# Two blocks of weights side by side: a decoder trunk whose half tiles change from 1024 rows of one block to 512 rows of two

## The chip, the cores and the metric

The kernel runs on one core of one Trainium2 chip. The metric is the device time of one execution in microseconds (us), the median of several runs. Matrix products run on TensorE, which reads weights and features from SBUF (the on-chip memory of 128 partitions) and adds into PSUM; VectorE and ScalarE do the elementwise work; SyncE (SP) issues the DMA transfers that bring the weights from HBM.

## What is computed

Two layers of a decoder trunk over 256 positions of width 2048, batch 1, in float32. Every product `a @ w` below is one of the matrix products that the change touches, save the small ones per pair of heads.

```
for l in range(DEPTH):                      # DEPTH = 2
    u = rms_norm(x, g_mix[l])
    cq_raw, ckv_raw, xb, yb, gate_a, gate_r = split_columns(u @ w_in[l])
    attn = mla_branch(cq_raw, ckv_raw, ...) # 16 heads, in 8 groups of two
    rec = rglru_branch(xb, yb, ...)         # conv, gates, a scan over positions, gelu
    merged = sigmoid(gate_a) * attn + sigmoid(gate_r) * rec
    x = x + merged @ w_out[l]
    hdn = square(relu(rms_norm(x, g_mlp[l]) @ w_up[l]))      # 8192 wide
    x = x + hdn @ w_down[l]
    x = x + sigmoid(rms_norm(x, g_ple[l]) @ w_ple_gate[l]) * (p[l] @ w_ple_proj[l])
return rms_norm(x, g_final)
```

## The kernel before

Features lie on the partitions and the 256 positions along the free axis. A feature tile is 128 features; the stream of 2048 is 16 such tiles (k = 0 to 15). Each activation is held twice, as a rounded part and the rest, side by side for each k in the buffers bufA and bufB; which buffer holds what alternates by stage. A weight is split in the same way, and three matmuls stand for one product of 128 x 128 weights with 256 positions: rounded x rounded, rounded x rest, rest x rounded (`mm3`, L221 to L223).

The weights come as one stream of 1,004 half tiles of 128 x 1024 (512 KB each), in the order in which they are used. A half tile of the large products holds 8 of the 16 k of one block of 128 output features. `load` (L102) issues one DMA for each on SP's queue into one of six raw buffers; `load_to` runs eight half tiles ahead of use, as far as buffers are free. `split_half` (L116) lets ScalarE round it (hi, L122) and VectorE take the rest (lo, L126), two half tiles ahead of use.

`mm_pair` computes two blocks into one PSUM bank of 512 columns, 256 for each. It takes four half tiles, `mm_half` 24 matmuls for each: first both halves of block 0, then both of block 1. For the first pair of most stages (`crossed`) the order is k 0 to 7 for block 0, the same for block 1, then k 8 to 15 for each, as the last features of the stage before come late. The last pair of a stage that must finish block by block goes through `mm_apart`, and single half tiles (the per-head projections, the embedding projection) are used as they are.

A small planner sets the order of everything else while the program is built: `later` enters a job (steps on VectorE, ScalarE, GpSimd with an estimated cost), `work` emits those that fit ahead of an estimated TensorE time, `need` forces a job when a matmul wants its result. Hooks between the half tiles of a pair place the norm's row sums (`root`, plain float32 matmuls into ms, L502), the broadcast of the norm's factor (`spread`, a plain float32 matmul into rb, L551) and the attention of the group before.

Stages per layer: c and kr (compressed queries and keys), 8 groups of xb, yb, gr, k, v, q, qr, lru, ga with the attention steps s, pt, o; then out (the output projection, whose input is merged by L1015 to L1024), four times up and down (the MLP), pp and pg (the embedding gate). In the profile's lines the tile written by a matmul has these names.

Of the kernel before, what the change touches and what calls it, by code (L numbers as in the profile page):

```python
# [18 lines left out]
P = 128  # L19
S = 256  # L20
D = 2048
KT = D // P
DEPTH = 2
HEADS = 16
GROUPS = HEADS // 2
D_FF = 8192
CHUNKS = D_FF // D
# [49 lines left out]
def trunk_kernel(ctx: ExitStack, tc: tile.TileContext, xT, pT, pos, par, gfin, invf, wu, out):  # L77
# [21 lines left out]
    nxt = {"dma": 0, "half": 0, "used": 0}  # L99
    LA, PD = 2, 8  # L100

    def load(h):  # L102
        t = wraw.tile([P, 1024], F32, tag="raw", name=f"raw{h}")
        nc.sync.dma_start(out=t, in_=wu[h])
        raws[h] = t

    def load_to(h):
# [75 lines left out]
    def need(key):  # L183

        if key not in done:
            next(j for j in jobs if key in j.keys).force()
        E["P"] = max(E["P"], done[key] + LATENCY)
# [31 lines left out]
    def mm3(o, wh, wl, ah, al, start, stop, shared=False):  # L219

        T.matmul(o, lhsT=wh, rhs=ah, start=start, stop=False, skip_group_check=shared)  # L221
        T.matmul(o, lhsT=wh, rhs=al, start=False, stop=False, skip_group_check=shared)  # L222
        T.matmul(o, lhsT=wl, rhs=ah, start=False, stop=stop, skip_group_check=shared)  # L223
        E["P"] += 0.328

    def mm_half(o, act, s, first=True, shared=False):


        hi, lo = half()
        for kk in range(8):  # L230
            k = 8 * s + kk
            need((act[1], k))
            c = slice(kk * P, (kk + 1) * P)
            mm3(o, hi[:, c], lo[:, c], act[0][:, k, 0, :], act[0][:, k, 1, :], first and k == 0, k == 15, shared)

    readers = {}

# [14 lines left out]
        for i in range(2):  # L252
            mm_half(ps[:, 0:S], act, i)

    def mm_pair(name, key, act, hooks=(), crossed=False):


        ps = mm_bank(name, key)
        for i in range(4):
            t, s = (i % 2, i // 2) if crossed else (i // 2, i % 2)  # L260
            mm_half(ps[:, t * S:(t + 1) * S], act, s, t == 0, True)
            if i < len(hooks) and hooks[i] is not None:
                hooks[i]()
        return ps
# [367 lines left out]
    def mixer(l, u, mg, norm):  # L632
        nl = Norm(f"c{l}", 512, 2, norm)
        raw, cn = {}, {}

        def dest(i, pr):
            raw[i, pr] = att.tile([P, 512], F32, tag="qk"[i] + "hl"[pr], name=f"raw{i}{pr}_{l}")
            return raw[i, pr]


        hooks = {1: (norm.root, None, None, norm.spread)} if l else {2: (None, norm.root), 3: (norm.spread,)}
        for n in range(4):
            i, pr = divmod(n, 2)
            key = ("c", i, pr, l)
            ps = mm_pair(f"c{i}{pr}_{l}", key, u, hooks.get(n, ()), n == 0)
            later(key, ("A", 0.6, lambda i=i, pr=pr, ps=ps: A.activation(dest(i, pr), ps, AF.Copy)), rank=-1)
            if l == n == 0:
                rope_tables()
                lru_constants()
            nl.squares((nl.name, "sq", n), lambda i=i, pr=pr: raw[i, pr], i, deps=(key,), last=pr == 1)  # L650


        kr = {}
        ps_k = mm_bank(f"kr_{l}", ("kr", l))
        mm_tile(ps_k, u)

        def evac_kr():
            kr["y"] = att.tile([P, S], F32, tag="oT", name=f"ykr_{l}")
            V.tensor_tensor(out=kr["y"], in0=ps_k[:, 0:S], in1=norm.R, op=ALU.mult)

        later(("kr", l), ("V", 0.38, evac_kr), deps=norm.factor(), rank=0)

        def normed():
            def steps(i, pr):
                d = {}

                def scale():
                    if i not in cn:
                        cn[i] = tuple(att.tile([P, 4, S], F32R, name=f"c{i}{w}_{l}", tag=f"c{i}{w}") for w in ("hi", "lo"))
                    d["v"] = raw[i, pr]  # L670
                    for t in range(2):
                        V.scalar_tensor_tensor(
                            out=d["v"][:, t * S:(t + 1) * S], in0=d["v"][:, t * S:(t + 1) * S],
                            scalar=param(l, ("g_q", "g_kv")[i], 2 * pr + t), in1=nl.R[:, i * S:(i + 1) * S],
                            op0=ALU.mult, op1=ALU.mult,
                        )

                def high():
                    A.activation(pair_of(cn[i][0], pr), d["v"], AF.Copy)

                def low():
                    V.tensor_tensor(out=pair_of(cn[i][1], pr), in0=d["v"], in1=f(pair_of(cn[i][0], pr)), op=ALU.subtract)

                return ("V", 0.8, scale), ("A", 0.52, high), ("V", 0.6, low)

            for i in (1, 0):
                for pr in range(2):
                    later(("cn", l, i, pr), *steps(i, pr), deps=nl.factor(), rank=0)

        def rot_kr():  # L690
            def sw():
                if "sw" not in kr:
                    kr["sw"] = t256(f"sw_k{l}")
                return kr["sw"]

            def split(d):
                return split_steps(d, f"krk{l}", lambda: d["t"], "kr", S)

            kr["rot"] = rotated(("rot", f"k{l}"), f"k{l}", lambda: kr["y"], lambda: kr["y"], sw, ("rope", ("kr", l)), split)

        def spread():
            nl.spread()
            normed()

        first = (nl.root, None, None, spread)
        for g in range(GROUPS):
            first = group(l, g, u, mg, norm, cn, kr, first, rot_kr if g == 0 else None)
# [334 lines left out]
    def residual(name, act, after):  # L1042

        def add(ps, xs):
            V.tensor_tensor(out=xs, in0=ps, in1=xs, op=ALU.add)

        for pr in range(8):
            if pr < 7:
                keys = (f"{name}_{pr}",)
                ps = mm_pair(f"{name}_{pr}", keys[0], act, (), pr == 0)  # L1050
                later(keys[0], ("V", 0.65, lambda ps=ps, pr=pr: add(ps, pair_of(x, pr))), rank=-1)
            else:
                keys = tuple((f"{name}_{pr}", t) for t in range(2))
                for t, ps in mm_apart(f"{name}_{pr}", keys, act):
                    later(keys[t], ("V", 0.38, lambda ps=ps, t=t: add(ps, x[:, 14 + t, :])), rank=-1)
            if after is not None:
                after(pr, keys)

    def mlp(l, a, hid, norm, after):
        for c in range(CHUNKS):  # L1060
            h_ = (hid, f"hid{l}_{c}")
            for pr in range(8):
                nm = f"{l}_{c}_{pr}"
                if c == CHUNKS - 1 and pr in (1, 5):
                    (ple_fetch, ple_rows)[pr // 5](l)
                ps_u = mm_pair(f"up{nm}", ("up", nm), a, BOUNDARY.get(8 * c + pr, lambda n: ())(norm), pr == 0)

                def steps(ps, pr, nm):
                    h, lo = parts(hid, pr)
# [30 lines left out]
    def ple(l, a, norm, after, hooks, by_tile=None):  # L1100
        need(("pe", l))
        ph, pl = (pe_in[w].rearrange("p (a s) -> p a s", s=S) for w in "hl")
        for pr in range(8):
# [42 lines left out]
                    after(pr, keys)  # L1146
            else:
                hook = BOUNDARY[pr](norm) if pr < 2 else hooks(pr)
                ps = mm_pair(f"pg{nm}", ("pg1", nm), a, hook, pr == 0)
                scale, tanh, mul, add = steps(ps, pps[pr % 2], pair_of(x, pr), lambda nm=nm: t512(f"pgt{nm}"))  # L1150
                later(("pg1", nm), ("V", 0.65, scale), deps=norm.factor(), rank=0)
                later(("pg", nm), ("A", 0.52, tanh), ("V", 0.6, mul), ("V", 0.6, add), deps=(("pg1", nm),))
# [227 lines left out]
```

## Time and profile before

| | us |
|---|---|
| median of 3 runs | 2925.97 (2925.73 to 2928.0) |
| profiled execution | 2925.61 |
| its span, first to last instruction | 2923.8 |
| TensorE busy (share of the span) | 2898.5 (99%) |
| VectorE busy | 1860.8 (64%) |
| ScalarE busy | 1536.2 (53%) |
| DMA, mean over the span | 183 GB/s |

The profile is one execution. Its busy times count an engine as busy from the start of an instruction to its modelled end, so for pipelined matmuls the distance between two starts says more than the duration of one. A stretch of the span is given by its start and end in us from the first instruction.

### The profile page before, as it was taken

To read this page: it belongs to the slowest core of one execution; us is meant where nothing else is said; L and a number is where in the kernel's file an instruction comes from. 1 tells how busy PE (TensorE), PEld (TensorE's weight loads), DVE (VectorE), ACT (ScalarE), POOL (GpSimd) and SP (SyncE) were. 2 spreads that over 40 slices of the span, in tenths; PEclk is the share of its full clock that TensorE was granted. 3 is DMA by queue.
4 is the path that set the end of the run, shared out by engine and by line. 5 is a ranking of instruction groups with operands and counts; after the bars stand their busy time and mean duration, and the time that the engine had idled before them with its cause. 6 is when DMAs were issued, how large, how long until landed. Compare 5 with 4: busy or idle time off the path is not lost. (4 is left out here: it accounts for less than half of the span.)

```text
span 2923.8 us, 58376 instructions
## 1 busy us (share of the span) xinstructions
PE 2898.5 (99%) x24800; PEld 2893.3 (99%) x24800; DVE 1860.8 (64%) x2420; ACT 1536.2 (53%) x2050; POOL 8.9 (0%) x17
## 2 busy tenths in 40 slices
PE   8999999999999999999999999999999999999998
PEld 8999999999999999999999999999999999999998
DVE  7877777765455554556758777777654555555565
ACT  5666666644344443444546666665443444434445
POOL 0000000000000000000000000000000000000000
PEclk9999999999999999999999999999999999999999
DMA  6555555555555555555555555555555555555553
GB/s 236 172 179 175 170 177 177 177 195 185 185 187 187 188 187 187 189 186 186 194 182 172 173 174 175 179 180 176 193 187 185 186 187 187 188 188 190 186 183 130
DMA packets 146998, 535.23 MB, mean 183 GB/s; under 512 B 16560, under 2 KB 16816, under 8 KB 146736
## 3 DMA queue, kind: packets, MB, share of 16 engines
q1 hardware_dynamic: 146736, 531.50, 55.2%
q8 instruction: 194, 3.18, 0.4%
q14 instruction: 68, 0.56, 0.0%
HBM read 529.33 MB, written 2.10 MB: 182 GB/s over the span
## 5 line engine op out<-in xcount | busy, mean ns | idle before, releaser
L122 ACT ACTIVATE hi<-raw 128x1024 fp32r<-128x1024 f32 x1004 | 1065.3, 1061 | 1358.5 <-PE down L222 412.0
L126 DVE TENSOR_TENSOR lo<-raw,hi 128x1024 fp32r<-128x1024 f32 x1004 | 1229.2, 1224 | 863.7 <-ACT hi L122 862.2
L221 PE MATMUL down<-bufB,hi 128*128 128x256 f32 x1024 | 287.7, 281 | 0.0
L222 PE MATMUL down<-bufB,hi 128*128 128x256 f32 x1024 | 287.7, 281 | 0.0
L223 PE MATMUL down<-bufB,lo 128*128 128x256 f32 x1024 | 287.7, 281 | 0.0
L221 PE MATMUL down<-bufA,hi 128*128 128x256 f32 x1024 | 287.7, 281 | 0.0
L222 PE MATMUL down<-bufA,hi 128*128 128x256 f32 x1024 | 287.7, 281 | 0.0
L223 PE MATMUL down<-bufA,lo 128*128 128x256 f32 x1024 | 287.7, 281 | 0.0
L221 PE MATMUL up<-bufA,hi 128*128 128x256 f32 x1024 | 287.7, 281 | 0.0
L221 PE MATMUL up<-bufB,hi 128*128 128x256 f32 x1024 | 287.7, 281 | 0.0
L223 PE MATMUL up<-bufA,lo 128*128 128x256 f32 x1024 | 287.5, 281 | 0.0
L223 PE MATMUL up<-bufB,lo 128*128 128x256 f32 x1024 | 287.5, 281 | 0.0
L222 PE MATMUL up<-bufA,hi 128*128 128x256 f32 x1024 | 287.5, 281 | 0.0
L222 PE MATMUL up<-bufB,hi 128*128 128x256 f32 x1024 | 287.5, 281 | 0.0
L222 PEld LDWEIGHTS down<-bufB,hi 128*128 128x128 f32 x1024 | 196.6, 192 | 0.0
L222 PEld LDWEIGHTS down<-bufA,hi 128*128 128x128 f32 x1024 | 196.6, 192 | 0.0
L222 PEld LDWEIGHTS up<-bufB,hi 128*128 128x128 f32 x1024 | 196.4, 192 | 0.0
L222 PEld LDWEIGHTS up<-bufA,hi 128*128 128x128 f32 x1024 | 196.4, 192 | 0.0
L221 PEld LDWEIGHTS up<-bufA,hi 128*128 128x128 f32 x1024 | 192.2, 188 | 0.0
L221 PEld LDWEIGHTS up<-bufB,hi 128*128 128x128 f32 x1024 | 192.2, 188 | 0.0
L223 PEld LDWEIGHTS up<-bufA,lo 128*128 128x128 f32 x1024 | 192.2, 188 | 0.0
L221 PEld LDWEIGHTS down<-bufB,hi 128*128 128x128 f32 x1024 | 192.2, 188 | 0.0
(551 smaller groups left out, 7839.1 us busy)
## 6 DMA issues: line engine op xcount, KB each, us to landing
raw<-wu SPq DMA_DIRECT2D x1004, 512.0 KB, 3.4
y<-rows SPq DMA_DIRECT2D x4, 512.0 KB, 4.0
x<-xT SPq DMA_DIRECT2D x3, 512.0 KB, 8.3
x<-xT SPq DMA_DIRECT2D x2, 256.0 KB, 4.9
praw<-pT SPq DMA_DIRECT2D x2, 256.0 KB, 4.7
parT<-par SPq DMA_DIRECT2D x1, 184.0 KB, 2.4
rope_w<-pos SPq DMA_DIRECT2D x1, 128.0 KB, 3.6
gf<-gfin SPq DMA_DIRECT2D x1, 8.0 KB, 8.3
```

Source lines behind the costliest of these rows:

```text
L122: A.activation(hi, src, AF.Copy)
L126: V.tensor_tensor(out=lo, in0=src, in1=f(hi), op=ALU.subtract)
L221: T.matmul(o, lhsT=wh, rhs=ah, start=start, stop=False, skip_group_check=shared)
L222: T.matmul(o, lhsT=wh, rhs=al, start=False, stop=False, skip_group_check=shared)
L223: T.matmul(o, lhsT=wl, rhs=ah, start=False, stop=stop, skip_group_check=shared)
```

## The change

A half tile of a pair now holds four k of both blocks: 512 columns of the one, 512 of the other. The array in HBM stays as it is; `plan` says for each half tile which pieces of which stored half tile it takes, and `load` issues one DMA per piece: one for the half tiles that stay as they were (`alone`), two of 256 KB for those of a pair. `mm_both` takes the place of `mm_half` in pairs: for each k, three matmuls for block 0 into columns 0 to 255, then three for block 1 into columns 256 to 511, on the same features. Every pair runs k from 0 to 15 in this order, so `crossed` goes. Only the first matmul of the bank carries the start flag, as before.

```diff
+    plan = []
+
+    def alone(n):
+        for _ in range(n):
+            plan.append(((len(plan), 0, 1024, 0),))
+
+    def pairs(n, crossed=False):
+        for _ in range(n):
+            b = len(plan)
+            for i in range(4):
+                plan.append(tuple(
+                    (b + (2 * (i // 2) + t if crossed else 2 * t + i // 2), 512 * (i % 2), 512, 512 * t) for t in range(2)
+                ))
+            crossed = False
+
+    for _ in range(DEPTH):
+        pairs(4, True)
+        alone(2)
+        for g in range(GROUPS):
+            pairs(3 if g == 0 else 2)
+            alone(4)
+            pairs(1 if g in (0, GROUPS - 1) else 2)
+            if g == GROUPS - 1:
+                alone(4)
+        pairs(7, True)
+        alone(4)
+        for _ in range(CHUNKS):
+            pairs(8, True)
+            pairs(7, True)
+            alone(4)
+        for i in range(4):
+            alone(1)
+            pairs(2 if i < 3 else 1, i == 0)
+        alone(4)
+
     def load(h):
         t = wraw.tile([P, 1024], F32, tag="raw", name=f"raw{h}")
-        nc.sync.dma_start(out=t, in_=wu[h])
+        for src, c, n, at in plan[h]:
+            nc.sync.dma_start(out=t[:, at:at + n], in_=wu[src, :, c:c + n])
         raws[h] = t
...
+    def mm_both(ps, act, i):
+
+        hi, lo = half()
+        for kk in range(4):
+            k = 4 * i + kk
+            need((act[1], k))
+            ah, al = (act[0][:, k, w, :] for w in range(2))
+            for t in range(2):
+                c = slice((4 * t + kk) * P, (4 * t + kk + 1) * P)
+
+                mm3(ps[:, t * S:(t + 1) * S], hi[:, c], lo[:, c], ah, al, k == t == 0, k == 15, True)
...
-    def mm_pair(name, key, act, hooks=(), crossed=False):
+    def mm_pair(name, key, act, hooks=()):
...
         for i in range(4):
-            t, s = (i % 2, i // 2) if crossed else (i // 2, i % 2)
-            mm_half(ps[:, t * S:(t + 1) * S], act, s, t == 0, True)
+            mm_both(ps, act, i)
             if i < len(hooks) and hooks[i] is not None:
                 hooks[i]()
```

## Rows read from the trace of the kernel before

**Rows 1.** The page's first part: busy us, share of the span, instructions.
```profile
PE 2898.5 (99%) x24800; PEld 2893.3 (99%) x24800; DVE 1860.8 (64%) x2420; ACT 1536.2 (53%) x2050; POOL 8.9 (0%) x17
```

**Rows 2.** Waits of TensorE: line, waited for, us in total, times, longest.
```profile
PE c L221 <- ACT hi L122: 8.5, 1, 8.5
...
PE out L222 <- DVE bufA L1024: 0.5, 1, 0.5
```

**Rows 3.** Table by stage: stretch, length, busy us and instructions per engine, PEclk, DMA share, GB/s.
```profile
0.00:540.00 540.00, 529.17 (x4525) 527.01 (x4526) 420.51 (x711) 354.26 (x550) 2.89 (x10) 1.00 0.55 183
540.00:650.00 110.00, 109.56 (x963) 109.36 (x962) 72.66 (x90) 55.89 (x72) 0.70 (x1) 1.00 0.57 187
650.00:1360.00 710.00, 710.00 (x6031) 709.95 (x6030) 381.11 (x372) 309.91 (x339) 0.00 (x0) 1.00 0.58 187
1360.00:1482.00 122.00, 122.00 (x1071) 121.89 (x1070) 83.58 (x106) 64.55 (x84) 1.40 (x2) 1.00 0.59 191
1482.00:1990.00 508.00, 506.08 (x4345) 504.27 (x4345) 384.79 (x605) 328.78 (x510) 1.86 (x1) 1.00 0.53 175
1990.00:2100.00 110.00, 109.47 (x964) 109.27 (x963) 72.12 (x89) 54.63 (x70) 0.70 (x1) 1.00 0.58 192
2100.00:2808.00 708.00, 708.00 (x6013) 707.95 (x6012) 380.16 (x371) 309.36 (x338) 0.00 (x0) 1.00 0.57 187
2808.00:2924.00 116.00, 104.21 (x904) 103.60 (x902) 65.91 (x79) 58.84 (x92) 1.39 (x2) 0.97 0.44 150
```

**Rows 4.** The same table for 80 us within layer 0's output projection.
```profile
560.00:640.00 80.00, 80.00 (x708) 80.00 (x707) 51.84 (x62) 42.29 (x54) 0.00 (x0) 1.00 0.59 193
```

**Rows 5.** Timeline of TensorE around the broadcast in layer 1's MLP: start us, duration us.
```profile
2102.38 0.28 PE L223 MATMUL up<-bufB,lo 128*128 128x256 f32 x1
...
2102.72 0.28 PE L223 MATMUL up<-bufB,lo 128*128 128x256 f32 x1
2102.84 0.59 PE L551 MATMUL rb_mlp<-dg_mlp,ones 128*128 128x256 f32 x2
...
2103.62 0.28 PE L221 MATMUL up<-bufB,hi 128*128 128x256 f32 x1
...
2103.97 0.28 PE L221 MATMUL up<-bufB,hi 128*128 128x256 f32 x1
```

**Rows 6.** Timeline of TensorE where the projection waits, layer 0 and layer 1.
```profile
555.55 0.28 PE L221 MATMUL out<-bufB,hi 128*128 128x256 f32 x1
556.27 0.39 PE L222 MATMUL out<-bufB,hi 128*128 128x256 f32 x1 [0.44 <-DVE bufB L1024]
...
2002.95 0.28 PE L221 MATMUL out<-bufA,hi 128*128 128x256 f32 x1
2003.76 0.39 PE L222 MATMUL out<-bufA,hi 128*128 128x256 f32 x1 [0.53 <-DVE bufA L1024]
```

**Rows 7.** Timeline of VectorE: the last step of the merged features 14 and 15.
```profile
555.80 0.75 DVE L1024 SCALAR_TENSOR_TENSOR bufB<-ga,bufB 128x256 fp32r<-128x256 f32 x2
```

**Rows 8.** Timeline of TensorE: first matmul of qr, of lru, and of what follows.
```profile
106.52 0.28 PE L221 MATMUL qr<-c0hi,hi 128*128 128x256 f32 x1
...
107.92 0.28 PE L221 MATMUL lru<-xc_0h,hi 128*128 128x256 f32 x1
...
109.32 0.28 PE L221 MATMUL ga<-bufA,hi 128*128 128x256 f32 x1
```

**Rows 9.** Issues of weights and of pT (ns min/median/max), landing, a stretch of the start.
```profile
L104 SPq DMA_DIRECT2D raw<-wu x1004: 327/328/432, 1.7 to 2887.5; - x168
DMA to landing us min/median/max: 3.0/3.4/9.1
...
L1095 SPq DMA_DIRECT2D praw<-pT x2: 425/426/426, 1190.0 to 2637.5; - x2
DMA to landing us min/median/max: 4.3/4.7/5.2
...
7.35:8.00 0.65, 0.00 (x0) 0.00 (x0) 0.00 (x0) 0.65 (x1) 0.00 (x0) 1.00 1.01 343
```

More of the change, by code (lines that the diff above doesn't have):

```diff
@@ L224, in mm3, with mm_half @@
         E["P"] += 0.328
-    def mm_half(o, act, s, first=True, shared=False):
+    def mm_half(o, act, s):
         hi, lo = half()
@@ L233, in mm_half @@
             c = slice(kk * P, (kk + 1) * P)
-            mm3(o, hi[:, c], lo[:, c], act[0][:, k, 0, :], act[0][:, k, 1, :], first and k == 0, k == 15, shared)
+            mm3(o, hi[:, c], lo[:, c], act[0][:, k, 0, :], act[0][:, k, 1, :], k == 0, k == 15)
+    def mm_both(ps, act, i):
[7 more added lines that the diff above has]
+                mm3(ps[:, t * S:(t + 1) * S], hi[:, c], lo[:, c], ah, al, k == t == 0, k == 15, True)
     readers = {}
@@ L644, in mixer @@
             key = ("c", i, pr, l)
-            ps = mm_pair(f"c{i}{pr}_{l}", key, u, hooks.get(n, ()), n == 0)
+            ps = mm_pair(f"c{i}{pr}_{l}", key, u, hooks.get(n, ()))
             later(key, ("A", 0.6, lambda i=i, pr=pr, ps=ps: A.activation(dest(i, pr), ps, AF.Copy)), rank=-1)
@@ L1049, in residual @@
                 keys = (f"{name}_{pr}",)
-                ps = mm_pair(f"{name}_{pr}", keys[0], act, (), pr == 0)
+                ps = mm_pair(f"{name}_{pr}", keys[0], act)
                 later(keys[0], ("V", 0.65, lambda ps=ps, pr=pr: add(ps, pair_of(x, pr))), rank=-1)
@@ L1065, in mlp @@
                     (ple_fetch, ple_rows)[pr // 5](l)
-                ps_u = mm_pair(f"up{nm}", ("up", nm), a, BOUNDARY.get(8 * c + pr, lambda n: ())(norm), pr == 0)
+                ps_u = mm_pair(f"up{nm}", ("up", nm), a, BOUNDARY.get(8 * c + pr, lambda n: ())(norm))
                 def steps(ps, pr, nm):
@@ L1148, in ple @@
                 hook = BOUNDARY[pr](norm) if pr < 2 else hooks(pr)
-                ps = mm_pair(f"pg{nm}", ("pg1", nm), a, hook, pr == 0)
+                ps = mm_pair(f"pg{nm}", ("pg1", nm), a, hook)
                 scale, tanh, mul, add = steps(ps, pps[pr % 2], pair_of(x, pr), lambda nm=nm: t512(f"pgt{nm}"))
```

## Prediction

> **What bounds the kernel now.** I read the busy shares first: TensorE is busy 99% of the span, VectorE 64%, ScalarE 53% [rows 1]. The view of waits says the same from the other side: after a first wait of 8.5 us for weights TensorE has only short ones, and those that the change can touch are half a microsecond at the start of each layer's output projection [rows 2]. So neither loads nor splitting are late, and the time is the number of matmuls times the distance between two starts. That distance is not one number. The table by stage gives it: both MLP stretches hold 6,031 matmuls in 710 us and 6,013 in 708 us, the stretches around the output projection 963 in 110 us [rows 3]. In 80 us within the projection stand 708 [rows 4]. Each count takes in about two matmuls already under way when the stretch begins, so the distances are 80/706 = 113.3 ns here and 710/6029 = 708/6011 = 117.8 ns in the MLP, at the same granted clock of 1.00, the level of 2.4 GHz. The kernel thus knows two levels, 4.5 ns apart, with the same instructions and shapes. What sets the level is what came last. The broadcast of a norm's factor (L551) shows it: three matmuls before it take 0.34 us, three after it 0.35 [rows 5], and the timeline shows the same behind all eight broadcasts; the slow level then lasts through the whole MLP. A stall can do the reverse: in layer 0 the projection begins at 0.353 us for three matmuls, waits at 556.27 for a feature, and is fast afterwards [rows 4, 6].
>
> **The matmuls.** Their number, shapes, weight loads and operands stay; only the order within two blocks changes. There are 218 pairs, 872 half tiles, so 872 x 8 = 6,976 groups of three. Each group now ends with a change of the output half of the bank, and every second time the same moving features come again. The nearest rows are the gates of the recurrence: tile lru does exactly this (three matmuls into one half, three into the other, on the same features), and the rope queries qr just before do not change the half at all. Both have 12 matmuls and both last 1.40 us [rows 8], and so it is in all 16 groups of heads. Within the 0.01 us of the timeline, over 16 places of four groups of three, that bounds the price of a change at about ±0.6 ns, or 6,976 x 0.6 = ±4.2 us. I take zero. What these rows do not show is whether either level survives the order, since lru runs at a third distance, 1.40/12 = 116.7 ns; that makes the first two rivals.
>
> **The waits.** Before, the first pair of a stage is crossed: features 0 to 7 for both blocks, then 8 to 15; features 14 and 15 are wanted at the end of the third half tile. After, the third half tile wants 8 to 11 and the fourth 12 to 15. Counted in matmuls of the stage, feature 14 is wanted at 2 x 24 + 18 = 66 before and at 3 x 24 + 12 = 84 after, which is 18 x 0.118 = 2.1 us later. VectorE's work on these two features ends at 555.80 + 0.75 = 556.55 [rows 7]; TensorE reached feature 14 at 555.55 and would now reach it at 557.7. The work is emitted by the planner's window and not by that need, so I leave it where it is, and both stalls go. They are 556.27 - 555.55 - 0.12 = 0.60 us in layer 0 and 2003.76 - 2002.95 - 0.11 = 0.70 in layer 1 [rows 6]. Sum: -1.3 us. What comes next there is nothing: features 8 to 13 were ready when they were wanted at matmul 48 and still are. If the work were emitted one half tile later, the stalls would stay, +1.3.
>
> **The level behind the stall.** Layer 0 enters the projection slow and only the stall made it fast. Without the stall I expect it slow until the norm's row sums (L502), behind which the timeline has the fast level each time. They follow the first pair of up: 8 x 96 matmuls of the projection, less the 66 before the stall, and 96 of up are 798, and 798 x 4.5 ns = +3.6 us. Layer 1 enters fast [rows 6] and stays so: 0.
>
> **The loads.** 132 half tiles keep one load, 872 get two of 256 KB with rows of 2 KB: 1,876 instead of 1,004. Issuing costs SP 0.328 us each [rows 9]; two are 0.66 us in the 24 x 0.118 = 2.83 us that a half tile lasts, so SP keeps up; behind it in the queue stand only the next loads. A load lands 3.4 us after issue, 9.1 at most; the two 256 KB transfers that run in the middle of the stream (pT) took 4.7 [rows 9]. The second half may thus land anything from 0 to 1.3 + 0.33 us later. A raw tile is loaded into the buffer that VectorE has freed and is split four half tiles later, 11.3 us: cover of 6 us and more, price 0; without that cover each half tile would cost what is missing. For throughput, in the first microseconds all 16 DMA engines are full, and the stretch in which x's 2 KB rows landed among others moved 343 GB/s [rows 9]; the stages need 173 to 192 [rows 3]. ScalarE waits for two loads per tile instead of one, while it is idle for almost half of the time [rows 1].
>
> The Trainium skill, page "SBUF — State Buffer", section "The DMA setup-cost knee", speaks against this part: every transfer pays about 2 us that do not depend on its size, so one should use the largest single transfer. By its figures two half loads would be an estimated 5.2 us if one waited for the other, more than a half tile lasts, and the kernel would become DMA-bound. The trace does not agree that they wait for each other: already now a load's 3.4 us is longer than the 2.83 us between loads [rows 9], and no matmul waits.
>
> **The start.** The first split waits for raw tile 0; it now comes in two loads, the second issued 0.33 us or a little more later, while DMA is full. Price 0 to 0.5 us on the 8.5 us wait [rows 2]; I take 0.2. In the half tiles after it fewer features must be ready, so nothing else is added.
>
> **Sum.** The profiled execution took 2925.6 us (span 2923.8). -1.3 + 3.6 + 0.2 = +2.5: 2928.1. The median of the runs is 0.4 above the profiled one, so 2928.5; I say 2928. Its own range: ±4.2 for the changed half, and half of rival 2's price in the attention stretches, ±4.5, since their level depends on what short matmuls left behind: 2921 to 2936.
>
> **Rival 1: the slow level does not hold.** If the new order, or a short stall by a late load, throws TensorE into the fast level in the MLP, each MLP saves 6,030 x 4.5 = 27 us: 2901 for one layer, 2874 for both. For it: nothing but history separates the levels, and one stall was enough in layer 0 [rows 6]. Against it: the slow level survived thousands of matmuls, changes of weight tile, of bank and of half, and the broadcast sets it anew in the same place.
>
> **Rival 2, on the slower side: the fast level does not hold.** If three matmuls of the alternating order cannot go below 0.353 us, each fast stretch pays 4.5 ns per matmul. From the counts at 117.8 ns [rows 3]: 540 to 650 becomes 113.2 (+3.2), 1360 to 1482 becomes 125.9 (+3.9), 1990 to 2100 +3.3, the last +2.1 above its busy time, the attention stretches +3.6 and +5.5: 21.6 in sum, of which the forecast's 3.6 is part. 2926.0 - 1.3 + 0.2 + 21.6 = 2946.5. It decides once about 1,560 of the fast matmuls are lost (7.0 us, of which the stalls give back 1.3). For it: the only rows with this order are at 116.7 ns. Against it: qr, without the order, is at 116.7 too.
>
> **Rival 3: DMA becomes the bound.** If a 2 KB row cost as much as one of 4 KB, the share would grow by 1876/1004 = 1.87: 0.58 becomes 1.08 and the MLP lasts 8% longer; over all stretches of [rows 3] some 150 us, 3075. Against it: 343 GB/s [rows 9].
>
> **Rival 4: the stalls stay** because the features come as late as they are wanted. Then layer 0 keeps its fast projection too: 2926.2.
>
> **How the numbers follow.** Forecast 0.66, rival 1 0.14 (half of it one layer), rival 2 0.13, rival 3 0.03, rival 4 0.04. The range takes in the forecast, one fast MLP and rival 2: 2899 to 2947. A measurement of this kernel can tell 0.2% from no change, that is 5.9 us. Faster: rival 1 and a small tail, 0.16. Slower: rivals 2 and 3 and that part of the forecast's own range which lies above 2931.9, 0.22. Same: 0.62.
>
> **What would show it.** Right: no wait of TensorE for the tiles of the merged features at the projection; 117.8 ns through both MLPs; layer 0's projection with some 680 matmuls in 80 us where it had 708; 1,876 loads at a DMA share below 0.7. Wrong: a distance in the MLP other than 117.8 ns, above all 113.3 or 116.7; fast stretches gone in the gates of the embedding stage (pg); TensorE waiting for split tiles.

## The result, and the profile after

The changed kernel takes 2884.32 us (median of 4 runs, 2883.93 to 2884.87) where the kernel before takes 2925.85 beside it (2924.45 to 2928.0): a ratio of 0.9858, with a 95% interval from 0.984 to 0.9875. The forecast was 2928, its range 2899 to 2947; the time lies 15 us below the range, ten above what rival 1 gave for two fast MLPs (2874). The span went from 2923.8 to 2882.2 us, 41.6 less.

The code lines have moved: the norm's row sums `ms`, L502 before, are L551 after, and the broadcast `rb`, L551 before, is L600 after; the three matmuls are L259 to L261.

Where the time went shows in the table by stage of the kernel after (stretch, length, busy us and instructions of TensorE, weight loads, VectorE, ScalarE, GpSimd, then PEclk, DMA share, GB/s), to be read against [rows 3]:

```profile
540.00:650.00 110.00, 110.00 (x938) 109.86 (x937) 73.30 (x101) 58.43 (x83) 0.00 (x0) 1.00 0.55 182
650.00:1340.00 690.00, 690.00 (x6084) 689.95 (x6084) 384.03 (x376) 312.48 (x341) 0.69 (x1) 1.00 0.59 194
1340.00:1460.00 120.00, 120.00 (x1052) 119.95 (x1051) 83.17 (x106) 63.22 (x83) 1.39 (x2) 1.00 0.58 193
1460.00:1970.00 510.00, 508.47 (x4371) 506.43 (x4370) 385.89 (x606) 329.09 (x508) 1.88 (x1) 1.00 0.53 175
1970.00:2080.00 110.00, 110.00 (x938) 110.00 (x937) 70.36 (x87) 55.01 (x72) 0.41 (x1) 1.00 0.56 184
```

The MLP of layer 0 holds 6,084 matmuls in 690 us, so 690/6082 = 113.5 ns each, where it had 117.8: 4.3 ns for some 6,030 matmuls, 26 us, and the same again in layer 1. The output projection went the other way: 938 matmuls in 110 us in both layers, where there had been 963 and 964. That is 25 and 26 distances of 0.1175 us more, 6.0 us in sum, and the stalls that the prediction took away are already counted in it. Two equal windows, one deep in the MLP and one in the projection, make this a plain count. Before:

```profile
670.00:1330.00 660.00, 660.00 (x5606) 660.00 (x5605) 351.95 (x341) 286.69 (x310) 0.00 (x0) 1.00 0.58 187
570.00:640.00 70.00, 70.00 (x620) 70.00 (x619) 45.83 (x56) 36.89 (x47) 0.00 (x0) 1.00 0.58 192
```

After:

```profile
670.00:1330.00 660.00, 660.00 (x5826) 660.00 (x5825) 366.46 (x356) 298.20 (x323) 0.00 (x0) 1.00 0.59 194
570.00:640.00 70.00, 70.00 (x597) 70.00 (x596) 42.97 (x50) 34.45 (x43) 0.00 (x0) 1.00 0.56 185
```

In the first window 660/5604 = 117.8 ns became 660/5824 = 113.3, in the second 113.3 became 117.6. The levels kept their sizes; they changed places. The timeline around the broadcast shows the exchange. TensorE, kernel after, layer 0's MLP (start us, duration us):

```profile
663.34 0.28 PE L259 MATMUL up<-bufA,hi 128*128 128x256 f32 x1
...
663.69 0.28 PE L259 MATMUL up<-bufA,hi 128*128 128x256 f32 x1
...
664.05 0.59 PE L600 MATMUL rb_mlp<-dg_mlp,ones 128*128 128x256 f32 x2
...
665.53 0.28 PE L259 MATMUL up<-bufA,hi 128*128 128x256 f32 x1
...
665.87 0.28 PE L259 MATMUL up<-bufA,hi 128*128 128x256 f32 x1
...
666.21 0.28 PE L259 MATMUL up<-bufA,hi 128*128 128x256 f32 x1
```

Three matmuls take 0.35 us ahead of the broadcast and 0.34 behind it, where it was 0.34 and then 0.35 in [rows 5]. The timeline has it so at all eight broadcasts: fast to slow before, slow to fast after. The row sums are the other half: the sums of those eight norms were each followed by the fast level before, and by the slow level after. They set it, whatever it was ahead of them. In the kernel before, the sums `ms_c` of layer 0 come behind matmuls at 117.8 ns (six take 0.71 us) and ahead of matmuls at 113.3 (0.68 us); in the kernel after it is the other way round:

```profile
69.45 0.28 PE L259 MATMUL xb<-bufA,hi 128*128 128x256 f32 x1
...
70.13 0.28 PE L259 MATMUL xb<-bufA,hi 128*128 128x256 f32 x1
...
70.47 0.95 PE L551 MATMUL ms_c<-ones,nacc_c 128*128 128x1 f32 x8
...
71.72 0.28 PE L259 MATMUL xb<-bufA,hi 128*128 128x256 f32 x1
...
72.43 0.28 PE L259 MATMUL xb<-bufA,hi 128*128 128x256 f32 x1
```

The sums of the MLP's norm in the kernel after come at the slow level and leave the slow level behind.

Beside the projection, the start is where time was lost. TensorE's waits after (line, waited for: us in total, times, longest):

```profile
PE c L259 <- ACT hi L160: 8.9, 1, 8.9
...
PE c L259 <- ACT bufA L629: 1.4, 1, 1.4
PE c L260 <- DVE bufA L633: 1.3, 2, 0.9
```

No wait at `out` is left in that view. The three new ones stand in the timeline of TensorE in the first pair:

```profile
18.55 0.28 PE L259 MATMUL c<-bufA,hi 128*128 128x256 f32 x1
19.23 0.38 PE L260 MATMUL c<-bufA,hi 128*128 128x256 f32 x1 [0.40 <-DVE bufA L633]
...
21.15 0.28 PE L261 MATMUL c<-bufA,lo 128*128 128x256 f32 x1
22.86 0.38 PE L259 MATMUL c<-bufA,hi 128*128 128x256 f32 x1 [1.43 <-ACT bufA L629]
24.12 0.38 PE L260 MATMUL c<-bufA,hi 128*128 128x256 f32 x1 [0.87 <-DVE bufA L633]
...
25.49 0.42 PE L259 MATMUL c<-bufA,hi 128*128 128x256 f32 x1
25.70 0.42 PE L260 MATMUL c<-bufA,hi 128*128 128x256 f32 x1
```

Less the usual 0.11, the three gaps are 0.57 + 1.60 + 1.15 = 3.3 us. Right behind them the matmuls start 0.21 us apart: the granted clock has gone from 2.4 to 1.2 GHz after these waits. The stretch from 26 to 60 us shows the mean of it, first before, then after:

```profile
26.00:60.00 34.00, 34.00 (x297) 33.95 (x295) 30.20 (x73) 18.26 (x25) 0.71 (x1) 1.00 0.58 190
```
```profile
26.00:60.00 34.00, 34.00 (x285) 33.95 (x285) 27.49 (x65) 19.66 (x28) 1.98 (x1) 0.96 0.50 166
```

A clock of 0.96 over 34 us is 1.4 us, and it is 0.96 over the 6 us before too (0.2). With 0.4 more on the first wait [rows 2] the start costs 3.3 + 1.4 + 0.2 + 0.4 = 5.3 us. The sum by these rows: 2925.6 - 52.0 + 6.0 + 5.3 = 2884.9; the profiled execution took 2883.9. Two of the start's terms are of this one execution. The first wait is anything from 8.0 to 8.9 us in the kernels of this study with the old first pair, so its 0.4 can't be put down to the change. And of the seven kernels with the new order in the first pair, all with much the same waits, the clock fell in four (0.95 to 0.97 between 26 and 60 us) and stayed at 1.00 in three: what decides it is not shown.

The loads did what the prediction said. The view of DMA issues after (count, KB each, median us to landing):

```profile
raw<-wu SPq DMA_DIRECT2D x1744, 256.0 KB, 3.0
raw<-wu SPq DMA_DIRECT2D x132, 512.0 KB, 3.3
```

### The profile page after: what moved, and what is told of

It is laid out like the page before. It is cut to its first block, busy times and chain, and to the rows that moved or that the text cites. A ratio compares the mean times of both kernels' runs of the same rounds, so it can differ in the third digit from the quotient of the medians.

```text
span 2882.2 us, 60564 instructions
## 1 busy us (share of the span) xinstructions
PE 2854.7 (99%) x24800; PEld 2849.0 (99%) x24800; DVE 1861.7 (65%) x2420; ACT 1536.8 (53%) x2050; POOL 10.1 (0%) x17
## 4 chain that ended last, share of the span: by engine, by line
PE 98%; ACT 1%; DMA 0%; DVE 0%; issue 0%; SPq 0%; ACTq 0%; POOLq 0%
PE up L259 8%; PE up L261 8%; PE up L260 8%; PE down L259 8%; PE down L260 8%; PE down L261 8%; PE out L261 2%; PE yb L261 2%; PE out L259 2%; PE out L260 2%; PE yb L259 2%; PE yb L260 2%; PE gr L259 2%; PE pg L259 2%; PE xb L259 2%; PE xb L261 2%
## 5 line engine op out<-in xcount | busy, mean ns | idle before, releaser
L259 PE MATMUL up<-bufA,hi 128*128 128x256 f32 x1024 | 283.2, 277 | 0.0
L259 PE MATMUL up<-bufB,hi 128*128 128x256 f32 x1024 | 283.2, 277 | 0.0
L260 PE MATMUL up<-bufA,hi 128*128 128x256 f32 x1024 | 282.9, 276 | 0.0
L260 PE MATMUL up<-bufB,hi 128*128 128x256 f32 x1024 | 282.9, 276 | 0.0
L261 PE MATMUL up<-bufA,lo 128*128 128x256 f32 x1024 | 282.9, 276 | 0.0
L261 PE MATMUL up<-bufB,lo 128*128 128x256 f32 x1024 | 282.9, 276 | 0.0
L259 PE MATMUL down<-bufB,hi 128*128 128x256 f32 x1024 | 282.6, 276 | 0.0
L260 PE MATMUL down<-bufB,hi 128*128 128x256 f32 x1024 | 282.6, 276 | 0.0
L261 PE MATMUL down<-bufB,lo 128*128 128x256 f32 x1024 | 282.6, 276 | 0.0
L259 PE MATMUL down<-bufA,hi 128*128 128x256 f32 x1024 | 282.6, 276 | 0.0
L260 PE MATMUL down<-bufA,hi 128*128 128x256 f32 x1024 | 282.6, 276 | 0.0
L261 PE MATMUL down<-bufA,lo 128*128 128x256 f32 x1024 | 282.6, 276 | 0.0
L261 PEld LDWEIGHTS up<-bufA,lo 128*128 128x128 f32 x1024 | 192.3, 188 | 0.0
L261 PEld LDWEIGHTS up<-bufB,lo 128*128 128x128 f32 x1024 | 192.3, 188 | 0.0
L259 PEld LDWEIGHTS up<-bufB,hi 128*128 128x128 f32 x1024 | 192.2, 188 | 0.0
L259 PEld LDWEIGHTS up<-bufA,hi 128*128 128x128 f32 x1024 | 192.2, 188 | 0.0
L259 PEld LDWEIGHTS down<-bufB,hi 128*128 128x128 f32 x1024 | 192.2, 188 | 0.0
```

## Experiments

In the first four kernels a switch chooses for each pair of blocks whether it has the old loads and order or the new. Three theories were tried on them. A: what counts is the level at which a stage is entered, and the vanished stall at the projection changed that. B: the order of the matmuls right behind sums and broadcast decides. C: the new order is itself faster in the MLP. The kernel before beside these four took 2924.48 us.

**The new order in the first pair of the projection alone.**

```diff
+def SIDE(name):
+    return name in ("out0_0", "out1_0")
```

> The kernel before, with the new order and loads in one pair per layer only: the first pair of the output projection. This takes the two stalls of 0.6 and 0.7 us away and leaves the rest as it was. Theory A (the level is carried: without the stall the projection stays at 117.8 ns, the row sums pass it on, and the broadcast turns it round): both MLPs at 113.3 ns, about 2926 - 1.3 + 7 - 54 = 2878 us. Theory B (the order of the matmuls right behind the row sums and the broadcast decides): projection at 117.8 ns in layer 0 at least, both MLPs still at 117.8 ns, about 2926 - 1.3 + 3.5 to 7 = 2928 to 2932 us.

2930.49 us. Both stalls are gone, the projection is slow in both layers (597 matmuls in the 70 us of the window above), the MLPs are slow (5,606). A falls.

**The new order in the pair of `up` that holds sums and broadcast, alone.**

```diff
+def SIDE(name):
+    return name in ("up0_0_1", "up1_0_1")
```

> The kernel before, with the new order and loads in one pair per layer only: the second pair of the MLP's first up chunk. It begins right behind the row sums, and the broadcast falls inside it. All else, 12,000 matmuls of the MLP among it, in the old order. Theory B: slow behind the row sums, fast behind the broadcast, so both MLPs at 113.3 ns in the old order, about 2926 - 54 = 2872 us. Theory A: no change, 2926 us, the MLPs at 117.8 ns. Theory C (the new order itself runs faster in the MLP): no change, 2926.

2925.26 us, MLPs slow. B falls.

**The changed kernel with that pair in the old order.**

```diff
+def SIDE(name):
+    return name not in ("up0_0_1", "up1_0_1")
```

> The changed kernel, with the old order and loads in that one pair per layer (the second of the first up chunk). Theory B: both MLPs at 117.8 ns although nearly all of their matmuls are in the new order, about 2884 + 54 = 2938 us. Theories A and C: no change, 2884 us.

2882.10 us, MLPs fast. B falls from the other side.

**The new loads with the old order inside a half tile:** twelve matmuls for one block, then twelve for the other.

```diff
-        for kk in range(4):
+        for t in range(2):
...
-            for t in range(2):
+            for kk in range(4):
```

> The changed kernel with its loads (512 rows of two blocks, two transfers per half tile), but within a half tile 12 matmuls for block 0 and then 12 for block 1, so that no group of three meets the same features as the group before it. If the loads or the removed stall bring the gain (theory A): 2884 us. If the alternation by threes brings it (theories B and C): the MLPs at 117.8 ns, about 2884 + 54 = 2938 us.

2886.44 us, with 5,826 matmuls in the window of the MLP, as in the changed kernel. The alternation by threes is not the cause: without it the MLP is just as fast. C falls for the alternation; for the new loads and the order of half tiles it falls with the run of the kernel before further down.

What the kernels with slow MLPs (before and the first two) have in common, and those with fast MLPs (after and the next two) too, is not in the work of TensorE: it has the same instructions in the same number ahead of every row sum. It is an address. `nacc`, the two tiles in which a norm adds its squares, is the stationary operand of the row sums. In the built programs it begins at byte 104608 of a partition in the first three and at 104640 in the other three, because the 32 bytes of `invf` were reserved behind it or ahead of it. Places are given in the order in which the program first names a tile, and the planner now comes to the squares later. First the kernel before, ScalarE's first square and SP's issue of invf (duration ns, start us twice):

```profile
L457 ACT ACTIVATE nacc_mix<-x x1: 617/617/617, 21.5 to 21.5; 128x512 f32<-128x512 f32 x1
...
L325 SPq DMA_DIRECT2D invf<-invf x1: 664/664/664, 23.3 to 23.3; - x1
```

and the kernel after:

```profile
L506 ACT ACTIVATE nacc_mix<-x x1: 622/622/622, 29.5 to 29.5; 128x512 f32<-128x512 f32 x1
...
L374 SPq DMA_DIRECT2D invf<-invf x1: 430/430/430, 24.5 to 24.5; - x1
```

Some tiles that take turns in the same buffers also stand in another of these, 2048 bytes or a multiple away. So the next theories were D: the place of these tiles sets the level behind the sums, and the broadcast turns it round; E: the stalls and the fallen clock of the start do it; F: the split loads as such.

**The kernel before, with the squares moved by 32 bytes and nothing else that TensorE reads:** invf, which only VectorE reads, is reserved at the top and no longer in `rope_tables`. In the built program every other tile has kept its address.

```diff
-        fr = const.tile([P, 1], F32, name="invf")
...
     hbx = const.tile([P, DEPTH, 16], F32, name="hbx")
+    fr = const.tile([P, 1], F32, name="invf")
```

> The kernel before, order and loads untouched; only the 32-byte constant invf is laid out ahead of the two tiles of squares (nacc) and not behind them, so that these begin at a multiple of 64 bytes (104640 in place of 104608), as they happen to do in the changed kernel. The row sums have these tiles as their stationary operand. Theory D (the place of these tiles decides which level follows a row sum, and the broadcast then turns it round): slow after the sums, fast after the broadcast, both MLPs at 113.3 ns, 2868 to 2882 us. Theory E (the stall and the clock's fall in the first 25 us of the changed kernel set it): MLPs stay at 117.8 ns, 2925 us. Theory F (the split loads as such): 2925 us.

2876.87 us beside 2928.39. Sums slow, broadcast fast at all eight places, and the window of the MLP is that of the changed kernel:

```profile
670.00:1330.00 660.00, 660.00 (x5826) 660.00 (x5825) 368.20 (x358) 298.38 (x325) 0.00 (x0) 1.00 0.60 195
```

E and F fall: no load, no order and no stall of the kernel before was touched. The same kernel in three rounds:

> The kernel before with the squares at 104640 alone, again, in three rounds for an interval. Theory D: 2875 to 2880 us, a ratio of 0.982 to 0.985; the changed kernel, at 0.986, then owes all of its gain and more to this place.

2875.97 us, a ratio of 0.9822 to the kernel before, 95% interval 0.9807 to 0.9837. The whole gain of the change, and some 8 us more, is to be had without the change.

The two profiles of this program, one from each of these two runs, do not agree level by level. In the stretch from 26 to 60 us the first has 297 matmuls and the second 293. And the stall at the start of layer 1's projection is in both, equally long. Behind it TensorE was slow in the first (596 matmuls in 70 us of the projection) and fast in the second (620):

```profile
1990.00:2060.00 70.00, 70.00 (x596) 70.00 (x596) 43.16 (x50) 34.45 (x43) 0.00 (x0) 1.00 0.56 187
```
```profile
1990.00:2060.00 70.00, 70.00 (x620) 70.00 (x619) 44.26 (x51) 35.56 (x44) 0.00 (x0) 1.00 0.58 193
```

So the program alone does not fix the level at every place: what a stall leaves behind, and so the level of the projection, may be another in the next execution. Behind the sums and the broadcasts the levels were the same in both, though the sums of layer 1's MLP came once at 117.8 ns and once at 113.3, and the MLPs were fast.

**The changed kernel, with the squares, the weights and the activations at the addresses of the kernel before.** (Some tiles that take turns in the same buffers still stand in another of these.)

```diff
     hbx = const.tile([P, DEPTH, 16], F32, name="hbx")
+    for i in range(2):
+        const.tile([P, 512], F32, tag="nacc", bufs=2, name=f"nacc_first_{i}")
```

> The changed kernel with the two tiles of squares laid out first, so that every tile stands at the very address that it had in the kernel before (squares at 104608, invf behind them at 108704). This repairs the run with squares at 104672, whose filler tiles also moved the weights by 64 bytes. Theory D (place of the squares): fast after the sums, slow after the broadcast, both MLPs at 117.8 ns; the change then shows its own worth at the old layout: 2926 + 5.5 at the start, less 1.3 of the stalls, plus up to 6.5 where the projection is slow, 2929 to 2938 us. If the place of the squares doesn't matter: 2884 us.

2932.82 us beside 2924.29, with 5,606 matmuls in the window:

```profile
670.00:1330.00 660.00, 660.00 (x5606) 660.00 (x5606) 350.58 (x338) 285.08 (x307) 0.00 (x0) 1.00 0.56 187
```

Sums fast, broadcast slow again. D holds both ways, and the table of four is complete: squares at 104608, 2924.3 without and 2932.8 with the change; squares at 104640, 2876.9 without and 2884.3 with it. By these four the change costs 8.5 us at the one place and 7.4 at the other. That it costs something is shown at 104640, where five runs without it (2873.5 to 2877.1) and four with it (2883.9 to 2884.9) do not meet; its size at 104608 is less sure, as that is one run against a kernel that ranged from 2924.3 to 2931.3 in its runs beside these experiments.

**The changed kernel with the first pair as before,** and invf reserved early so that the squares keep their place.

```diff
+def SIDE(name):
+    return name != "c00_0"
...
+    fr = const.tile([P, 1], F32, name="invf")
```

> The changed kernel with the first pair of the program (c00 of layer 0) in its old loads and crossed order, and invf laid out early so that the squares keep their place at a multiple of 64. Theory D: MLPs fast, and the 5 to 6 us lost at the start come back: 2876 to 2880 us. Theory E: without the stalls of the start the MLPs are slow, 2922 to 2932 us. Theory F: 2879 to 2884 us, as D.

2877.99 us. The MLPs are fast without the stalls of the start, against E, and the start is mended: the clock is 1.00 again between 26 and 60 us.

```profile
26.00:60.00 34.00, 34.00 (x293) 33.95 (x292) 29.68 (x71) 17.87 (x24) 0.71 (x1) 1.00 0.58 192
```

The 6.3 us between this and the changed kernel are the new order in one pair out of 218; what is left of the change in the other 217 is 1.1 us against the run with the squares alone, in one run each, less than the 3.7 us by which the five runs with the squares alone differ among themselves.

**The reverse, with filler tiles:** the changed kernel with the squares at 104672.

```diff
     hbx = const.tile([P, DEPTH, 16], F32, name="hbx")
+    const.tile([P, 1], F32, name="pad0")
...
+                    const.tile([P, 1], F32, tag="pad1", name=f"pad1_{self.name}")
                     self.R = const.tile([P, S], F32, tag="R", name=f"R_{self.name}")
```

> The changed kernel, with two unused tiles of 32 bytes, one ahead of invf and one behind the tiles of squares, so that the squares begin at 104672, 32 bytes past a multiple of 64, and all that lies behind them keeps its place relative to 64 bytes. Theory D: fast after the sums, slow after the broadcast, both MLPs slow, 2925 to 2940 us. Theories E and F: no change, 2884 us.

2974.67 us, 35 more than the most that a theory gave. The fillers had also moved the split weights by 64 bytes, and the window of the MLP held 5,562 matmuls: 118.7 ns, a distance that no stage of the kernel before has. That opened the second question, theory G: what counts is how weights and moving activations lie to each other.

**Weights 64 bytes further, squares unmoved,** in the changed kernel:

```diff
-                    self.R = const.tile([P, S], F32, tag="R", name=f"R_{self.name}")
+                    self.R = const.tile([P, S + 16], F32, tag="R", name=f"R_{self.name}")[:, 0:S]
```

> The changed kernel with 64 unused bytes ahead of the raw weights; the split weights begin at a multiple of 128 (134400) as the activations do, the squares stay at 104640. Theory G: 118.7 ns in every stage fed from the two activation buffers, no levels any more, 2968 to 2978 us. If the squares made the surplus of the run with squares at 104672: 2884 us.

2975.49 us; the squares had nothing to do with it:

```profile
670.00:1330.00 660.00, 660.00 (x5562) 659.95 (x5561) 348.19 (x335) 283.36 (x307) 0.00 (x0) 1.00 0.56 185
```

**The same with 32 bytes** (`S + 8`):

> The changed kernel with 32 unused bytes ahead of the raw weights: weights at 96 past a multiple of 128, activations at 0. Theory G in steps of 64 bytes: as the changed kernel, 2884 us, or as the run with 64 bytes more, 2973 us. If the keys' distance of 116.7 ns (their tiles are 32 bytes off) is what any pair 32 bytes off gives: 116.7 ns everywhere, 2930 to 2940 us.

2961.85 us and 5,626 matmuls in the window, 117.4 ns; the attention's tiles moved by 32 with it. Layer 1's MLP ran at another distance in the same execution, 610/5141 = 118.7 ns:

```profile
2170.00:2780.00 610.00, 610.00 (x5143) 610.00 (x5142) 319.51 (x305) 258.65 (x276) 0.00 (x0) 1.00 0.56 186
```

None of the three numbers expected.

**Every tile that TensorE reads at a multiple of 64,** first pair old:

```diff
-    power = const.tile([P, 4], F32, name="power")
+    power = const.tile([P, 16], F32, name="power")[:, 0:4]
...
+    fr = const.tile([P, 16], F32, name="invf")[:, 0:1]
...
     xbuf = att.tile([P, 2, 260], F32, name="xbuf")
+    att.tile([P, 8], F32, name="pad0")
```

> As the run beside it with the first pair old, and every tile that TensorE reads begins at a multiple of 64 bytes (the tiles of the projections, keys, queries and values began 32 bytes past one). By the distances of the kernel before, the products on those tiles (116.7 ns, about 1250 of them besides the values) come to 113.3: 4 us less. If the places of stationary tiles turn the level also at the attention's products, the slow stretches of xb, yb and out (some 4200 distances at 117.8) may change as well: 2850 to 2880 us; if not, 2872 to 2877 us.

2964.98 us: the weights had come to 134400, as in the run with 64 bytes more, and the window of the MLP to 5,564. Tidy addresses as such are no remedy.

**The same, and the weights 64 further:** R with `S + 16`.

> As the run with every tile at a multiple of 64, with 64 bytes more ahead of the weights, so that the split weights begin at 64 past a multiple of 128 (as in both first kernels) and the activations at a multiple of 128. Theory G (weights and activations whose places agree modulo 128 cost 118.7 ns a matmul, places 64 apart 113.3 or 117.8): 118.7 is gone everywhere, 2840 to 2880 us. If alignment of the projections' and values' tiles as such made that run slow: 2960 us again.

2927.93 us. 118.7 ns is gone everywhere, as G says, though the time lies above the 2880 that was its most. The projection is fast (620 in the 70 us), but the MLPs are slow (5,606), although the squares lie at a multiple of 64. Was it their place modulo 128 (theory H)?

```diff
-    fr = const.tile([P, 16], F32, name="invf")[:, 0:1]
+    fr = const.tile([P, 32], F32, name="invf")[:, 0:1]
```

> As the run with every tile at 64 and the weights 64 bytes past a multiple of 128, with 64 more unused bytes ahead of the squares, which now begin at 104768, 64 past a multiple of 128, as the weights do (before: 104704, a multiple of 128); all other tiles keep their places modulo 128. The old first pair is kept. Theory H (squares 64 past a multiple of 128: slow after the sums, fast after the broadcast; at any other place the reverse or slow after both): MLPs fast and, as the projection there was fast too, 2852 to 2876 us. If the alignment of the attention's tiles fixed the level in the MLP instead: 2928 us.

2927.82 us, ratio 0.9998 (0.9989 to 1.0008), level by level as the run before it. H falls: the place of the squares decides only together with something else.

The same layout with the old loads and order:

```diff
 def SIDE(name):
-    return name != "c00_0"
+    return False
```

> The very layout of the run beside it, with the old loads and the old order in every pair: what the change itself brings at one layout. By the sum of the prediction (stalls at the projection 1.3 us, all else nothing) it is 1 to 2 us slower than the run beside it; if loads by two blocks cost something in the steady state, faster by that.

2935.58 us, 1.0026 (1.0016 to 1.0037). Here the change without its first pair gains 7.8 us, not the 1 to 2 expected: by the sum of its distances 3.9 in each projection, which is slow from its stall on in the old order (597 in the window) and fast in the new (620).

What else differed between this layout and the one with fast MLPs were the weights (128 bytes further) and the attention's tiles (32). Three runs from the kernel before with the squares at 104640, beside 2925.76 us, tell them apart.

**Weights 128 further** (`S + 32`):

> The kernel before with the squares at 104640, and 128 unused bytes ahead of the raw weights: every tile behind them, the weights, the diagonals and the attention's tiles among them, keeps its place modulo 128 and changes it modulo 256. If the weights' place modulo 256 took the fast level from the MLPs in the run with everything at 64: MLPs slow, 2920 to 2932 us. If it was the alignment of the attention's tiles: no change, 2877 us.

2945.41 us, above what either case said, MLPs slow:

```profile
670.00:1330.00 660.00, 660.00 (x5606) 660.00 (x5605) 350.89 (x338) 285.94 (x309) 0.00 (x0) 1.00 0.58 187
```

**The attention's tiles alone 32 further:**

```diff
     xbuf = att.tile([P, 2, 260], F32, name="xbuf")
+    att.tile([P, 8], F32, name="pad0")
```

> The kernel before with the squares at 104640, and 32 unused bytes behind xbuf alone, so that the attention's tiles begin at multiples of 64 while weights, squares and diagonals stay where they were. If the alignment of the attention's tiles took the fast level from the MLPs: slow MLPs, 2925 to 2936 us. If it was the weights' place modulo 256: fast MLPs, and the products on those tiles 3.3 ns a matmul shorter, 2868 to 2875 us.

2869.31 us, the shortest time of this study (one run), with fast MLPs (5,826) and, not foreseen, a fast projection behind its stall. As a stall can leave either level behind, the projection's part is not put down to the tiles:

```profile
670.00:1330.00 660.00, 660.00 (x5826) 660.00 (x5825) 367.88 (x358) 298.24 (x325) 0.00 (x0) 1.00 0.59 195
570.00:640.00 70.00, 70.00 (x620) 70.00 (x619) 46.31 (x55) 36.81 (x47) 0.00 (x0) 1.00 0.60 194
```

The products on the attention's tiles came to the fast distance: qr and lru take 1.36 us for 12 matmuls, 113.3 ns, where [rows 8] have 1.40.

```profile
104.65 0.28 PE L221 MATMUL qr<-c0hi,hi 128*128 128x256 f32 x1
...
106.01 0.28 PE L221 MATMUL lru<-xc_0h,hi 128*128 128x256 f32 x1
...
107.37 0.28 PE L221 MATMUL ga<-bufA,hi 128*128 128x256 f32 x1
```

**Weights 192 further** (`S + 48`), at the same place modulo 256 as the activations:

> The kernel before with the squares at 104640, and 192 unused bytes ahead of the raw weights, so that the split weights agree with the activations modulo 256 (134528 and 32896, both 128) and modulo 128. Theory G in steps of 128: 118.7 ns in every stage fed from the activation buffers, 2965 to 2976 us, as with 64 more bytes. If the conflict goes by 256 bytes: 113.3 or 117.8 ns, 2850 to 2930 us.

2998.68 us, above both ranges, at a further distance, 660/5498 = 120.0 ns:

```profile
670.00:1330.00 660.00, 660.00 (x5500) 659.95 (x5500) 343.18 (x329) 279.21 (x301) 0.00 (x0) 1.00 0.56 183
```

## Why the prediction was wrong, point by point

**Two levels, set by what came before: right, and not deep enough.** 113.3 and 117.8 ns hold in the new order to the tenth.

**The half change and the second use of the features, taken at zero of ±4.2 us: right.** With and without the alternation the window of the MLP holds 5,826 matmuls.

**The stalls, -1.3 us: right.** No wait at the projection is left, in either layer, and none came in its place.

**The loads, 0: right.** After the first pair TensorE waits for no split tile. The 256 KB loads land 3.0 us after issue, the 512 KB ones 3.3, and 3.4 before [rows 9]. That agrees with the Trainium skill, page "SBUF — State Buffer", section "The DMA setup-cost knee", in that most of the landing does not go with the size; the bound on the kernel that the prediction worked out from it did not come, as the loads overlap: 1,744 of 3.0 us, one behind the other, would be 5.2 ms, against a span of 2.9.

What did change is out of TensorE's sight. ScalarE's idle time before a rounding, ended by matmuls of up and down in the kernel before, is now ended by the loads more than by anything else, 459 of 1316 us (us in total, times, longest):

```profile
ACT hi L160 <- DMA raw<-wu: 458.7, 278, 1.8
```

**The level behind the stall: half right.** Layer 0's projection is slow without its stall, as the prediction said. "Layer 1 enters fast and stays so" failed: it is slow as well. With the changed order at the old addresses it is layer 0 that is fast and layer 1 that is slow, so the level at this place followed from nothing that the prediction had in hand, and that layer 0 came out as said owes something to luck. The reading under it, that a stall makes TensorE fast, failed too: the same stall left the slow level and the fast one in two executions of one program.

**The start: the mis-sized term, 0.2 against 5.3 us.** "In the half tiles after it fewer features must be ready, so nothing else is added" is the sentence that failed. It is true of the need and wrong of the order: the planner forces a feature's split when a matmul needs it; needed later, it was emitted later, and TensorE came to features of the later half tiles before they were split, three times. ScalarE rounds the last of the 16 features here, first before, then after:

```profile
16.85 1.29 ACT L580 ACTIVATE bufA<-x,parT 128x256 fp32r<-128x256 f32 x3
```
```profile
22.32 1.69 ACT L629 ACTIVATE bufA<-x,parT 128x256 fp32r<-128x256 f32 x4
```

In this execution the clock fell behind the waits. At the old addresses the waits came as well, the clock stayed at 1.00, and the kernel took 2932.8 us where 2928 was forecast, inside the forecast's own range of 2921 to 2936.

**"The broadcast sets it anew in the same place": the step that failed.** Eight of eight broadcasts made TensorE slow, and I read that as the broadcast setting the slow level. It turned the level round in both kernels, though in the run that moved only the squares its own operands stayed where they were; what set it were the row sums, and what these set changed when their stationary operand moved by 32 bytes. The prediction said that the operands of the matmuls stay. Their contents did; one address did not, and the diff doesn't show it. This gave the 52 us; start and projections took 11 back.

**The rivals.** Rival 1 had the outcome, two fast MLPs, and 2874; by its mechanism, the order or a late load, it was wrong: order, loads and stalls each left the level of the MLPs alone. The 10 us between its number and the time are the start (5.3), layer 1's projection (3.8: the 26 distances of 0.1175 us and the stall of 0.70 that the forecast had already taken off), and small things. Rivals 2 and 3 did not come: fast stretches stayed as fast, and the DMA share in the MLP is 0.59. Rival 4 did not either.

## What to carry to other kernels

Before a difference of a per cent or two is put down to an edit, compare the addresses of the operands in both programs, and run the old kernel at the new addresses: here that one line separated a layout worth -50 us from a change worth +8 (at these two layouts; at a third, without its first pair, it was worth -8). A transition that looks the same eight times (fast to slow) does not say whether an event sets a state or turns it; that takes a case in which the state ahead of it is different. And where work is emitted by need, a later need is a later emission.

## What the runs showed of the hardware

The distance of these matmuls (moving 256 columns of 4 bytes, stationary 128 x 128, clock 1.00) depends on where the operands lie in SBUF, with steps at 32 and 64 bytes and a difference between places 128 bytes apart. With the weights' address less the activations' taken modulo 256, the MLP ran at 113.3 or 117.8 ns for 64 (before, after, and the runs without moved weights), 117.4 in layer 0 and 118.7 in layer 1 for 96, 118.7 for 128, 117.8 for 192 in all four runs there, and 120.0 for 0. From best to worst that is 6% of the distance, and 2869 to 2999 us for the same instructions. Whether it is the difference alone was not separated from the places themselves, since the fillers moved all tiles behind them, among them the diagonals that the broadcast reads; nor is it shown why a broadcast turns the level or how the place of the squares reaches matmuls that do not read them. At 192 the sums and the broadcast both leave the slow level, while the projection can be fast. So D holds at the two layouts where it was tried, and is no rule for others.

The Trainium skill, page "SBUF — State Buffer", section "Operand start alignment", asks of an operand's place only that it be a multiple of the element size; that is about what is read, and in these runs the distance of the matmuls goes by the place as well. Its page "TensorE: Matmul & The Clock Gate", section "Back-to-back issue gap", gives columns / 2.4 + 2.5 for the distance of isolated warm matmuls, an estimated 109.2 ns here. No stage of any of these runs with 256 columns was below 113.3.
